# Feed-forward of a mixture of experts in halves of 1792 columns instead of quarters of 896, with two weight blocks of each half multiplied whole in float32

## The chip, the cores and the metric

The kernel runs on one core of one Trainium2 chip. The metric is the device time of one execution, in microseconds (us); lower is better.

## What is computed

Two layers over 272 tokens of width 1024 (16 fixed tokens ahead of the 256 of the input). Layer 0 ends in a dense feed-forward, layer 1 in a mixture of eight experts. The change touches the mixture alone:

```python
def swiglu(h, wg, wu, wd):
    return (jax.nn.silu(h @ wg) * (h @ wu)) @ wd

def moe_swiglu(h, router, wg, wu, wd):      # h: (1, 272, 1024); wg, wu: (8, 1024, 3584); wd: (8, 3584, 1024)
    logits = jnp.einsum('bld,de->ble', h, router).astype(jnp.float32)
    top_vals, top_idx = lax.top_k(logits, 2)
    top_w = jax.nn.softmax(top_vals, axis=-1)
    combine = jnp.sum(jax.nn.one_hot(top_idx, 8) * top_w[..., None], axis=-2)
    out = jnp.zeros_like(h)
    for e in range(8):
        out = out + combine[..., e:e + 1] * swiglu(h, wg[e], wu[e], wd[e])
    return out
```

The output is `rmsnorm(h + f)` of the last 256 tokens. All arrays are float32. Only those 256 tokens go through the mixture.

## The kernel before

**Precision.** TensorE is fed float32r, a rounded form of float32. Each weight block is therefore split in two: ScalarE (ACT) copies the raw block into a rounded first part (`whi`, line 149, `first_parts`), VectorE (DVE) subtracts it from the raw block and so makes the rest (`wlo`, line 157, `second_parts`). TensorE multiplies the tokens by both (`stream`, line 1089). The tokens of an expert are gathered into 128 places by a matmul with a selection matrix (`gather`, line 1028, plain float32). An expert with 64 tokens or fewer (few) has the rounded part of its tokens in the first 64 places of `exh` and the rest of them in the other 64, so that one pass over `whi` and `wlo` covers both; a small matmul by `fold` (line 1064) adds the lower half of the sums to the upper. An expert with more tokens (many) has all places filled, and after each unit of two blocks a branch (`tc.If(many > 0)`, line 1168) runs extra matmuls of `exl`, the tokens' rest, by `whi` (lines 1185 and 1205).

**Tiling.** The 3584 columns of an expert are done in `NS = 4` slabs of 896. A slab has four blocks of the gate and four of the up matrix (256 rows x 896 columns each, two row chunks side by side, so 1792 columns per partition), then the four blocks of the down matrix of the slab before (256 rows x 1024; the last 128 rows). Gate and up sums stand in a pair of PSUM banks each (`pgate`, `pup`), from a pool of three pairs (`rot`); the down sums of an expert stand in a pair of their own (`y`). When a sum is complete, ACT copies it to `part` for the fold (line 1060), TensorE folds, ACT computes Silu (line 1212), DVE the product with the up sums (line 1216); TensorE transposes the product (line 1075), and ACT and DVE split it again (`hh`, `hl`).

**Order.** Inside the mixture the order on TensorE, ACT and DVE is the program's. `unit` (line 1154) runs two blocks; at block m it first issues the first part of block m + 3 and the second part of block m + 1 (m + 2 for the last ten), and after a block it runs what `then(m, ...)` has hung there: folds, Silu, product, the gather of the next expert. Weight blocks are loaded by SyncE (line 101) into seven raw slots, in order; a slot is free once DVE has made the second part (`freed`). There are seven slots for `whi` and five for `wlo` (`NHI`, `NLO`).

**The end.** An expert's output is weighed into `yout` (`keep`, line 1095) and written to DRAM (`ydram`); in the last expert, `rows` (line 1136) gathers for each token the rows of the other seven from there, and DVE adds them to the residual `hsum` (line 1139).

Of the kernel before, what the change touches and what calls it, by code (L numbers as in the profile page):

```python
# [36 lines left out]
NSC = SLAB // P  # L37
ZROW = (NE - 1) * CAP
# [22 lines left out]
class Weights:  # L61
# [3 lines left out]
    def __init__(self, nc, blocks, slots):  # L65
# [11 lines left out]
        self.n_small = sum(blk[1] for blk in blocks[:self.first])  # L77
        self.n_hi = self.n_lo = 0
# [66 lines left out]
    def first_parts(self, j):  # L145
        while self.n_hi < min(j + 1, self.n_large):
            w, shaped = self.large(self.n_hi)
            hi = shaped(self.slot(self.n_hi % NHI, f"whi{self.n_hi}"))
            self.nc.scalar.activation(hi, w, AF.Copy)  # L149
            self.his[self.n_hi] = hi  # L150
            self.n_hi += 1

    def second_parts(self, j):
        while self.n_lo < min(j + 1, self.n_large):
            w, shaped = self.large(self.n_lo)
            lo = shaped(self.slot(NHI + self.n_lo % NLO, f"wlo{self.n_lo}"))
            self.nc.vector.tensor_sub(lo, w, self.his[self.n_lo].bitcast(F32))  # L157
            self.los[self.n_lo] = lo
            self.freed(self.first + self.n_lo)
            self.n_lo += 1  # L160
# [3 lines left out]
def tile_block(ctx, tc, x, meta_tokens, rel_bias, w_in, pool_group_w, w_pool_up, w_attn_up, w_out, dense_w_gate,  # L164
# [68 lines left out]
    def add_up(w, e, s):  # L233
        for b in range(4):
            src = w[0, e, b * 256:b * 256 + 256, s * SLAB:(s + 1) * SLAB]
            blocks.append((src.rearrange("(k p) f -> p k f", p=P), 1, None))

    def add_down(e, s, c0, m):
        for b in range((NSC + 1) // 2):
            r = s * SLAB + b * 256  # L240
            n = min(2, NSC - 2 * b)
            src = moe_w_down[0, e, r:r + n * P, c0:c0 + m]
            blocks.append((src.rearrange("(p k) f -> p k f", k=n), 1, None))
# [724 lines left out]
    def places():  # L968
        nc.vector.scalar_tensor_tensor(posb, few[:, None].to_broadcast([P, 2, NE]), float(HALF), pos, op0=ALU.mult,
                                       op1=ALU.add)  # L970

    def tables(pc_):
# [4 lines left out]
        nc.vector.tensor_scalar(big2, few, -1.0, 1.0, op0=ALU.mult, op1=ALU.add)  # L977
# [24 lines left out]
    exl = act.tile([P, 2, NCH, CAP], F32R, name="exl", tag="xl")  # L1002

    class Expert:


        def __init__(self, e):
# [9 lines left out]
            self.xh, self.xl = exh[:, e % 2], exl[:, e % 2]  # L1017
# [5 lines left out]
        def gather(self, cs=range(NCH)):  # L1023
            if cs[0] == 0:
                self.pg = two("pgat").rearrange("p h (c s) -> p (h c) s", s=CAP)
# [14 lines left out]
        def scales(self):  # L1040
            self.pst = bank("pst")
# [13 lines left out]
    def folded(E, ps):  # L1055
# [6 lines left out]
        def add():  # L1062
            for hf in range(2):
# [3 lines left out]
    def chunk(ci):  # L1067

        b, i = ci // 2, ci % 2
        return slice(b * 256 + i, (b + 1) * 256, 2) if ci < NSC - 1 else slice(b * 256, SLAB)  # L1070

    def turn(hs):
        pt = two("pth").rearrange("p h (c s) -> p (h c) s", s=P)[:, 0:NSC]
        for ci in range(NSC):
            nc.tensor.transpose(pt[:, ci], hs[:, chunk(ci)], ident)
        return pt
# [77 lines left out]
    def unit(bs, run, extra, many):  # L1154

        held = []
        m0 = step[0]
        for b in bs:
            m = step[0]
            ws.first_parts(m + AHEAD)  # L1160
            ws.second_parts(m + (1 if m < ws.n_large - 10 else 2))
            held.append(ws.his.pop(m))
            run(b, (held[-1], ws.los.pop(m)))
            if b != bs[-1]:
                for f in hooks.pop(m, ()):
                    f()
                step[0] += 1
        with tc.If(many > 0):  # L1168
            for b, hi in zip(bs, held):
                extra(b, hi)  # L1170
        for f in hooks.pop(step[0], ()):
            f()
        step[0] += 1

    def up(E, name):
        ps = two(name)
        outs = [(ps[:, hf, 0:SW], slice(hf * SW, (hf + 1) * SW)) for hf in range(2)]

        def run(b, parts):
            stream(outs, parts, [E.xh[:, 2 * b], E.xh[:, 2 * b + 1]], b == 0, b == 3)  # L1180

        def extra(b, hi):
            for i in range(2):
                for o, f in outs:
                    nc.tensor.matmul(o, E.xl[:, 2 * b + i], hi[:, i, f], start=False, stop=True, skip_group_check=True)

        for bs in ((0, 1), (2, 3)):
            unit(bs, run, extra, E.many)
        return ps[:, :, 0:SW]

    def down(E, s, h, hfs=(0, 1)):
# [4 lines left out]
        def chunks(b):  # L1196
            return range(2 * b, min(2 * b + 2, NSC))

        def run(b, parts):
            stream(outs, parts, [h[0][:, ci] for ci in chunks(b)], s == 0 and b == 0, s == NS - 1 and b == 3)  # L1200

        def extra(b, hi):
            for i, ci in enumerate(chunks(b)):
                for o, f in outs:
                    nc.tensor.matmul(o, h[1][:, ci], hi[:, i, f], start=False, stop=True, skip_group_check=True)

        for bs in ((0, 1), (2, 3)):
            unit(bs, run, extra, E.many)

    def gated(E, pg_, gs2, add):  # L1210
# [254 lines left out]
```

## Time and profile before

| | |
|---|---|
| three runs | 1563.52, 1564.65, 1564.68 us; median 1564.65 |
| profiled execution | 1566.1 us, its span 1564.3 us |
| mean granted TensorE clock | 0.986 of full speed |
| busy share of the span | TensorE matmul 94%, weight loads 82%, DVE 83%, ACT 69% |
| moved by DMA | 460.98 MB, mean 295 GB/s |

The mixture begins at about 616 us of the span and takes the rest of it. A stretch is read by its own rows: a matmul's duration includes the pipeline and overlaps the next, so that TensorE's pace is the distance from one start to the next, not the mean duration. A plain float32 matmul is recorded as two matmuls.

### The profile page before, as it was taken

The page shows a single profiled execution, that of the slowest core. Times are in us where ns is not written, and L with a number is a line of the kernel's source. Part 1 is how long each engine was busy: PE and PEld are TensorE (multiplying, and loading weights), DVE is VectorE, ACT ScalarE, POOL GpSimd, SP SyncE. Part 2 cuts the span into 40 slices and gives each one's busy share as a digit, 9 for nine tenths or more (in the row PEclk, how much of TensorE's full clock was granted, in tenths as well). Part 3 has the DMA queues.
Part 4 walks back from the last instruction along what each step waited for, and adds up shares of the span by engine and source line. Part 5 has one row for each costly group of instructions (what it writes and reads, how often), then busy time and mean ns, then how long its engine had stood idle before and what let it go on. Part 6 is the DMA issues. An engine that isn't in the chain of part 4 may idle for free. (4 is left out here: it accounts for less than half of the span.)

```text
span 1564.3 us, 22760 instructions
## 1 busy us (share of the span) xinstructions
PE 1469.2 (94%) x8667; PEld 1277.6 (82%) x8667; DVE 1306.1 (83%) x1429; ACT 1072.1 (69%) x1067; POOL 20.2 (1%) x27
## 2 busy tenths in 40 slices
PE   8999999999999997899899999999999999998785
PEld 7989999999999997677677888888776677676563
DVE  7766776666678677799999988878999999999896
ACT  5455554444455645878888767866888888887875
POOL 1000000000000000000000000000000000000100
PEclk9999999999999998999999999999999999999988
DMA  9734454555564336799999999999999999999994
GB/s 307 244 129 136 162 189 169 182 168 183 165 193 136 126 118 237 252 386 409 407 408 408 386 317 355 362 329 331 390 405 410 408 407 409 408 407 405 394 401 152
DMA packets 181266, 460.98 MB, mean 295 GB/s; under 512 B 10378, under 2 KB 83256, under 8 KB 169240
## 3 DMA queue, kind: packets, MB, share of 16 engines
q1 hardware_dynamic: 177328, 449.97, 77.5%
q0 software_dynamic: 2688, 9.24, 1.5%
q8 instruction: 81, 1.33, 0.3%
q14 instruction: 41, 0.34, 0.1%
q10 hardware_dynamic: 1128, 0.11, 0.1%
HBM read 453.49 MB, written 5.80 MB: 294 GB/s over the span
## 5 line engine op out<-in xcount | busy, mean ns | idle before, releaser
L157 DVE TENSOR_TENSOR wlo<-raw,whi 128x1792 fp32r<-128x1792 f32 (+2 forms) x388 | 753.1, 2001 | 28.0 <-ACT whi L149 25.1
L149 ACT ACTIVATE whi<-raw 128x1792 fp32r<-128x1792 f32 (+2 forms) x388 | 639.6, 1681 | 81.4 <-DMA raw<-in_moe_w_gate_dram 28.4
L125 ACT ACTIVATE w<-raw 128x1024 fp32r<-128x1024 f32 x180 | 189.7, 1058 | 251.1 <-PE ps L440 185.4
L126 DVE TENSOR_TENSOR w<-raw,w 128x1024 fp32r<-128x1024 f32 x180 | 219.5, 1223 | 66.4 <-ACT w L125 66.0
L440 PE MATMUL ps<-xh,w 128*128 128x272 f32 (+1 forms) x896 | 177.0, 293 | 0.5 <-ACT hT L761 0.5
L440 PE MATMUL ps<-fh,w 128*128 128x272 f32 x864 | 164.5, 290 | 0.0
L1089 PE MATMUL pgate<-wlo,exh 128*128 128x448 f32 x512 | 132.9, 382 | 22.5 <-DVE wlo L157 21.8
L440 PEld LDWEIGHTS ps<-xh,w 128*128 128x128 f32 x896 | 142.4, 190 | 4.2 <-PE s L502 1.1
L1089 PE MATMUL pgate<-whi,exh 128*128 128x448 f32 x512 | 133.0, 382 | 5.3 <-DVE exh L1036 1.8
L440 PEld LDWEIGHTS ps<-fh,w 128*128 128x128 f32 x864 | 135.7, 188 | 0.0
L1089 PE MATMUL pup<-whi,exh 128*128 128x448 f32 x512 | 127.8, 371 | 7.1 <-PEq L1168 6.0
L1089 PE MATMUL y<-wlo,hh 128*128 128x512 f32 x434 | 127.1, 408 | 6.8 <-DVE wlo L157 3.5
L1089 PEld LDWEIGHTS pgate<-wlo,exh 128*128 128x128 f32 x512 | 95.7, 193 | 44.6 <-DVE wlo L157 37.2
L1089 PE MATMUL pup<-wlo,exh 128*128 128x448 f32 x512 | 127.8, 371 | 2.2 <-DVE wlo L157 2.0
L440 PE MATMUL ps<-xl,w 128*128 128x272 f32 (+1 forms) x448 | 126.8, 288 | 0.0
L1089 PE MATMUL y<-whi,hh 128*128 128x512 f32 x434 | 122.8, 399 | 4.2 <-PEq L1168 1.5
L440 PE MATMUL ps<-fl,w 128*128 128x272 f32 x432 | 124.2, 288 | 0.0
L1089 PEld LDWEIGHTS pup<-whi,exh 128*128 128x128 f32 x512 | 95.0, 189 | 23.4 <-issue 13.7
L1089 PEld LDWEIGHTS y<-wlo,hh 128*128 128x128 f32 x434 | 77.0, 188 | 44.7 <-DVE wlo L157 30.0
L1089 PEld LDWEIGHTS pgate<-whi,exh 128*128 128x128 f32 x512 | 94.5, 193 | 20.9 <-issue 11.0
L1089 PEld LDWEIGHTS pup<-wlo,exh 128*128 128x128 f32 x512 | 93.5, 188 | 17.8 <-DVE wlo L157 10.3
L1089 PEld LDWEIGHTS y<-whi,hh 128*128 128x128 f32 x434 | 79.6, 188 | 27.3 <-issue 6.1
(315 smaller groups left out, 1995.3 us busy)
## 6 DMA issues: line engine op xcount, KB each, us to landing
raw<-in_moe_w_gate_dram SPq DMA_DIRECT2D x128, 896.0 KB, 8.9
raw<-in_moe_w_up_dram SPq DMA_DIRECT2D x128, 896.0 KB, 9.4
raw<-in_moe_w_down_dram SPq DMA_DIRECT2D x93, 1024.0 KB, 9.4
raw<-in_w_in_dram SPq DMA_DIRECT2D x30, 1024.0 KB, 6.3
raw<-in_moe_w_down_dram SPq DMA_DIRECT2D x37, 512.0 KB, 7.9
raw<-in_dense_w_gate_dram SPq DMA_DIRECT2D x14, 1024.0 KB, 5.0
raw<-in_dense_w_up_dram SPq DMA_DIRECT2D x14, 1024.0 KB, 4.9
raw<-in_dense_w_down_dram SPq DMA_DIRECT2D x14, 1024.0 KB, 5.0
```

What stands on the lines that cost most here:

```text
L125: self.nc.scalar.activation(hi, w, AF.Copy)
L126: self.nc.vector.tensor_sub(lo, w, hi.bitcast(F32))
L149: self.nc.scalar.activation(hi, w, AF.Copy)
L157: self.nc.vector.tensor_sub(lo, w, self.his[self.n_lo].bitcast(F32))
L440: newest[0] = nc.tensor.matmul(ps, w_[part][:, k, ms_], xp[:, k, sl], start=t == 0 and k == 0, stop=t == 2 and k == nk - 1).ins
L1089: nc.tensor.matmul(ps, x_, part[:, i, f], start=first and i == 0 and part is parts[0], stop=last and i == len(chunks) - 1 and part is part ...
```

## The change

- `NS` is 2: a half has 1792 columns. A gate or up block is now 128 rows x 1792 columns, eight of each to a half (as many bytes per block as before, one run of 7168 bytes per partition in place of two of 3584). A half has seven down blocks of 256 rows.
- The first gate and the first up block of each half are not split. They are multiplied from the raw block in plain float32, by `xf`, a float32 copy of the first 128 rows of the gathered tokens; no extra matmul runs for them. Their raw slot is free only when TensorE is done (`freed` in `unit`).
- Sums of a half need four PSUM pairs: `pgate0`, `pgate1`, `pup0`, `pup1`, from the same pool of three; `pup1` takes the pair of `pgate0`, and Silu of `pgate0` is done in two parts. The first up unit runs its two blocks piece by piece with the fold and Silu of `pgate0` in between.
- `NLO` is 4, second parts are always made two blocks ahead. The tail's `rows` and their additions are hung at other places.

The core of the diff:

```diff
-NS = 4
+NS = 2
-NRAW, NRAWE, NPAIR, NHI, NLO, AHEAD = 6, 2, 5, 7, 5, 3
+NRAW, NRAWE, NPAIR, NHI, NLO, AHEAD = 6, 2, 5, 7, 4, 3
-SLAB = DFF // 4
-SW = SLAB // 2
+SLAB = DFF // 2
+SW = SLAB // 4
...
     def add_up(w, e, s):
-        for b in range(4):
-            src = w[0, e, b * 256:b * 256 + 256, s * SLAB:(s + 1) * SLAB]
-            blocks.append((src.rearrange("(k p) f -> p k f", p=P), 1, None))
+        for b in range(NCH):
+            src = w[0, e, b * P:(b + 1) * P, s * SLAB:(s + 1) * SLAB]
+            blocks.append((src.rearrange("(k p) f -> p k f", p=P), 1 if b else 0, None))
...
         def first(self, cs=slice(0, NCH)):
             nc.scalar.activation(self.xh[:, cs], self.pg[:, cs], AF.Copy)
+            if cs.start == 0:
+                nc.scalar.activation(self.xf[:, 0:HALF], self.pg[:, 0, 0:HALF], AF.Copy)
+                nc.scalar.activation(self.xf[:, HALF:], self.pg[:, 0, HALF:], AF.Copy,
+                                     scale=big2[:, self.e:self.e + 1])
...
+    def unit(bs, runs, extra, many):
+        m0 = step[0]
         held = []
         for b in bs:
+            m = m0 + b - bs[0]
             ws.first_parts(m + AHEAD)
-            ws.second_parts(m + (1 if m < ws.n_large - 10 else 2))
+            ws.second_parts(m + 2)
+            if m in ws.whole:
+                held.append((ws.large(m)[0], None))
+            else:
+                held.append((ws.his.pop(m), ws.los.pop(m)))
+            if len(runs) == 1:
+                runs[0](b, held[-1])
+                if m in ws.whole:
+                    ws.freed(ws.first + m)
...
+        if len(runs) > 1:
+            for run in runs:
+                run(bs, held)
+            for i in range(len(bs)):
+                if m0 + i in ws.whole:
+                    ws.freed(ws.first + m0 + i)
...
+        def block(b, parts, outs):
+            w, lo = parts
+            if lo is None:
+                for o, f in outs:
+                    nc.tensor.matmul(o, E.xf, w[:, 0, f], start=b == 0, stop=b == NCH - 1)
+            else:
+                stream(outs, parts, [E.xh[:, b]], b == 0, b == NCH - 1)
...
+                runs = [some(outs[0:2], 0), call(between[0]), some(outs[0:2], 1), call(between[1])]
+                for o in outs[2:4]:
+                    runs += [some([o], 0), some([o], 1)]
+            unit((b, b + 1), runs, extra, E.many)
...
+            if end:
+                then(mg + 2, lambda: added.append(rows(0)))
+                then(mg + 7, lambda: (added[0](), added.append(rows(1))))
+                then(mg + 11, lambda: added[1]())
+            pg_ = [two("pgate0"), two("pgate1")]
+            up(E, sums(pg_[0], 0) + sums(pg_[1], 1))
...
+            def first_gate(E=E, ps=pg_[0], gs2=gs2[0], add=add_g):
+                for hf in range(2):
+                    gated(E, ps, gs2, add, (hf,))
...
+            up(E, sums(pu[0], 0) + sums(pu[1], 1), (first_gate, lambda: None))
...
+            if prev is None:
+                turn_part(0, md)
+                turn_part(1, md + 1)
+            else:
+                then(md + 3, lambda f=turn_part: f(0, md + 4))
+                if end:
+                    then(md + 5, lambda f=turn_part: f(1, mt))
+                down(prev[0], prev[1], turned)
+                if not end:
+                    turn_part(1, mt)
+                if prev[1] == NS - 1:
+                    add_y = folded(prev[0], prev[0].y)
+                    then(mt + 1, add_y)
+                    then(mt + 2, lambda E=prev[0]: keep(E, E.e))
```

How the order moves, at the two places that the prediction speaks of. The first is the step from the last gate block to the first up unit, in the middle of the mixture. TensorE before, the end of the first up unit and the fold of the gate sums behind it:

```order
L1089 MATMUL pup<-whi_8762,exh 128x448 [waits Activation_49]
L1089 MATMUL pup<-whi_8762,exh 128x448 x3
L1089 MATMUL pup<-wlo_8805,exh 128x448 [waits DVE_49]
L1089 MATMUL pup<-wlo_8805,exh 128x448 x3
L1168 COMPARE_AND_BRANCH
L1185 MATMUL pup<-whi_8739,exl 128x448 x4
L1185 MATMUL pup<-whi_8762,exl 128x448 x4
L1168 UNCONDITIONAL_BRANCH
L1168 UNCONDITIONAL_BRANCH [waits PE_49]
L1064 MATMUL pgate<-part,fold 128x448 [waits Activation_49]
L1064 MATMUL pgate<-part,fold 128x448
```

TensorE with the change, the first up unit itself (`pup_8931` is `pup0`, `pup_8932` is `pup1` in the banks of `pgate_8790`, which is `pgate0`):

```order
L1208 MATMUL pup_8931<-raw_8796,exf 128x448 [waits DMAHW3_49,PE_49]
L1208 MATMUL pup_8931<-raw_8796,exf 128x448
L1074 MATMUL pgate_8790<-part,fold 128x448 [waits Activation_49] x2
L1099 MATMUL pup_8931<-whi_8897,exh 128x448 x2
L1099 MATMUL pup_8931<-wlo_8909,exh 128x448 [waits DVE_49]
L1099 MATMUL pup_8931<-wlo_8909,exh 128x448
L1208 MATMUL pup_8932<-raw_8796,exf 128x448 [waits Activation_49]
L1099 MATMUL pup_8932<-whi_8897,exh 128x448
L1099 MATMUL pup_8932<-wlo_8909,exh 128x448
L1208 MATMUL pup_8932<-raw_8796,exf 128x448
L1099 MATMUL pup_8932<-whi_8897,exh 128x448
```

ACT before, at the same step (`part` is the copy of the gate sums, `gs` is Silu):

```order
L1060 ACTIVATE part<-pgate 128x2x448
L149 ACTIVATE whi_10574<-raw_10449 128x1792
L1168 UNCONDITIONAL_BRANCH
L149 ACTIVATE whi_10588<-raw_10495 128x2048
L1212 ACTIVATE gs<-pgate,rcs 128x896
```

ACT with the change:

```order
L1070 ACTIVATE part<-pgate_8790 128x2x448 [waits PE_49]
L154 ACTIVATE whi_8935<-raw_8829 128x1792 [waits DMAHW5_49,DVE_49]
L154 ACTIVATE whi_8941<-raw_8843 128x1792 [waits DMAHW6_49,DVE_49]
L1254 ACTIVATE gs<-pgate_8790,rcs 128x448 [waits PE_49] x2
L1070 ACTIVATE part<-pgate_8791 128x2x448 [waits Activation_49]
```

ACT's order is the same, with two first parts between `part` and Silu. What moved is TensorE: before, nothing of the up block waited for Silu; now the first matmul into `pup1` waits for ACT in the middle of the unit.

The second place is the last expert, where the gathered rows are added to the residual. ACT before (`yout<-y` is the output of expert 6):

```order
L149 ACTIVATE whi_14279<-raw_14192 128x1792
L1095 ACTIVATE yout<-y,rcs 128x1024
L149 ACTIVATE whi_14304<-raw_14218 128x1792
L1168 UNCONDITIONAL_BRANCH
L149 ACTIVATE whi_14318<-raw_14232 128x1792
```

DVE before, up to the first two additions:

```order
L1079 TENSOR_TENSOR hl<-pth,hh 128x896
L1081 SCALAR_TENSOR_TENSOR hh<-hl,few,hh 128x7x64
L157 TENSOR_TENSOR wlo_14528<-raw_14403,whi_14479 128x1792
L157 TENSOR_TENSOR wlo_14551<-raw_14429,whi_14510 128x1792
L157 TENSOR_TENSOR wlo_14565<-raw_14443,whi_14526 128x1792
L1168 UNCONDITIONAL_BRANCH
L157 TENSOR_TENSOR wlo_14592<-raw_14469,whi_14549 128x1792
L157 TENSOR_TENSOR wlo_14606<-raw_14483,whi_14563 128x1792
L1139 TENSOR_TENSOR hsum<-hsum,yout 128x1024
L1168 UNCONDITIONAL_BRANCH
L1139 TENSOR_TENSOR hsum<-hsum,exl 128x1024
```

ACT with the change:

```order
L154 ACTIVATE whi_14008<-raw_13894 128x1792
L154 ACTIVATE whi_14022<-raw_13911 128x1792
L154 ACTIVATE whi_14043<-raw_13942 128x1792
L1105 ACTIVATE yout<-y,rcs 128x1024
L1193 UNCONDITIONAL_BRANCH
```

DVE with the change:

```order
L163 TENSOR_TENSOR wlo_14063<-raw_13942,whi_14043 128x1792
L1193 UNCONDITIONAL_BRANCH
L163 TENSOR_TENSOR wlo_14086<-raw_13977,whi_14061 128x1792
L163 TENSOR_TENSOR wlo_14098<-raw_14012,whi_14084 128x1792
L1193 UNCONDITIONAL_BRANCH
L163 TENSOR_TENSOR wlo_14131<-raw_14026,whi_14119 128x1792
L1193 UNCONDITIONAL_BRANCH
L1149 TENSOR_TENSOR hsum<-hsum,yout 128x1024
L1149 TENSOR_TENSOR hsum<-hsum,exl 128x1024
```

With the change three second parts stand between the one that belongs to the first part ahead of `yout` (`whi_14043`) and the first addition. Before, there are thirteen between the one that belongs to the first part behind `yout` (`whi_14304`) and the first addition.

## Rows read from the trace of the kernel before

**Rows 1.** Busy time by stretch: us, then PE, PEld, DVE, ACT, POOL, clock, DMA, GB/s.

```profile
1131.07:1404.76 273.69, 251.76 (x1148) 192.94 (x1147) 269.98 (x171) 238.33 (x169) 1.06 (x2) 1.00 1.02 408
866.01:1122.57 256.56, 254.31 (x1237) 221.04 (x1236) 216.95 (x137) 189.17 (x135) 1.06 (x2) 1.00 0.94 349
616.00:650.00 34.00, 27.57 (x121) 23.13 (x122) 21.46 (x29) 17.97 (x14) 0.51 (x1) 0.89 0.47 157
```

**Rows 2.** Timeline of ACT: Silu of two slabs, ten apart; output of two experts, two apart.

```profile
1131.07 1.01 ACT L1212 ACTIVATE gs<-pgate,rcs 128x896 f32<-128x896 f32 x1
...
1404.76 0.99 ACT L1212 ACTIVATE gs<-pgate,rcs 128x896 f32<-128x896 f32 x1
...
866.01 1.10 ACT L1095 ACTIVATE yout<-y,rcs 128x1024 f32<-128x1024 f32 x1
...
1122.57 1.12 ACT L1095 ACTIVATE yout<-y,rcs 128x1024 f32<-128x1024 f32 x1
```

**Rows 3.** DMA packets, 1217 to 1227 us (gate, up), then 1208 to 1212 us (down).

```profile
DMA packets 1196, 4.04 MB, mean 404 GB/s; under 512 B 68, under 2 KB 68, under 8 KB 1196
...
DMA packets 231, 1.69 MB, mean 422 GB/s; under 512 B 25, under 2 KB 25, under 8 KB 25
```

**Rows 4.** Timeline of DVE: seven second parts in a row (start, us).

```profile
1513.43 13.90 DVE L157 TENSOR_TENSOR wlo<-raw,whi 128x1792 fp32r<-128x1792 f32 x7
```

**Rows 5.** TensorE groups, 1131.07 to 1404.76 us: count, busy us, mean ns, idle before.

```profile
L1089 PE MATMUL y<-wlo,hh 128*128 128x512 f32 x140 | 41.1, 409 | 1.6 <-DVE wlo L157 0.5
...
L1089 PE MATMUL pgate<-wlo,exh 128*128 128x448 f32 x160 | 40.8, 377 | 7.6 <-DVE wlo L157 7.3
...
L1028 PE MATMUL pgat<-s,h2g 128*128 128x128 f32 x96 | 11.2, 275 | 0.0
L1075 PE MATMUL pth<-cst,gs 128*128 128x128 f32 x70 | 10.7, 292 | 1.5
```

**Rows 6.** Timeline of TensorE in an expert with many tokens.

```profile
910.12 1.79 PE L1185 MATMUL pup<-whi,exl 128*128 128x448 f32 x8
911.75 0.57 PE L1064 MATMUL pgate<-part,fold 128*128 128x448 f32 x2
...
920.75 2.03 PE L1205 MATMUL y<-whi,hl 128*128 128x512 f32 x8
922.62 0.57 PE L1064 MATMUL pup<-part,fold 128*128 128x448 f32 x2
```

**Rows 7.** Timeline of TensorE across the end of a unit, an expert with few tokens.

```profile
1527.65 0.99 PE L1089 MATMUL pup<-wlo,exh 128*128 128x448 f32 x4
1528.79 1.17 PE L1089 MATMUL y<-whi,hh 128*128 128x512 f32 x4
```

**Rows 8.** Timeline of TensorE: plain float32 matmuls, 16 of 128 columns, one of 272.

```profile
1144.69 3.74 PE L1028 MATMUL pgat<-s,h2g 128*128 128x128 f32 x32
...
27.33 0.62 PE L411 MATMUL pr<-ss,ones 128*128 128x272 f32 x2
```

**Rows 9.** Timeline of ACT after the last gate block, an expert with many tokens.

```profile
907.08 0.92 ACT L1060 ACTIVATE part<-pgate 128x896 fp32r<-128x896 f32 x1 [3.95 <-PE pgate L1185]
907.89 3.50 ACT L149 ACTIVATE whi<-raw 128x1792 fp32r<-128x1792 f32 x2
912.35 1.01 ACT L1212 ACTIVATE gs<-pgate,rcs 128x896 f32<-128x896 f32 x1 [0.96 <-PE pgate L1064]
```

**Rows 10.** From the output of expert 6 to its gathered rows: ACT, POOL; median us to landing.

```profile
1453.33 1.11 ACT L1095 ACTIVATE yout<-y,rcs 128x1024 f32<-128x1024 f32 x1
...
1464.35 3.07 POOL L1136 DMA_INDIRECT yout<-ydram,rows_of  x1 [9.06 <-DMA ydram<-yout]
1467.72 2.58 POOL L1136 DMA_INDIRECT exl<-ydram,rows_of  x1 [0.30 <-issue]
...
yout<-ydram,rows_of POOLq DMA_INDIRECT x2, 9.2
exl<-ydram,rows_of POOLq DMA_INDIRECT x2, 9.0
```

More of the change, by code (lines that the diff above doesn't have):

```diff
@@ L77, in __init__ @@
         self.n_small = sum(blk[1] for blk in blocks[:self.first])
+        self.whole = {j for j, blk in enumerate(blocks[self.first:]) if blk[1] == 0}
+        self.parted = [j for j in range(self.n_large) if j not in self.whole]
         self.n_hi = self.n_lo = 0
@@ L1069, in chunk, with turn @@
         b, i = ci // 2, ci % 2
[L1070 to L1075, printed above, removed]
+        return slice(b * 256 + i, (b + 1) * 256, 2)
+    def turn(hs, cis):
+        pt = two("pth").rearrange("p h (c s) -> p (h c) s", s=P)[:, 0:len(cis)]
+        for i, ci in enumerate(cis):
+            nc.tensor.transpose(pt[:, i], hs[:, chunk(ci)], ident)
         return pt
@@ L1175, in up @@
[L1175 to L1180, printed above, removed]
-        def extra(b, hi):
[L1183 to L1189, printed above, removed]
+            ws.second_parts(m + 2)
@@ new lines, in unit, with up, some, call @@
+        with tc.If(many > 0):
+            for b, (hi, lo) in zip(bs, held):
+                if lo is not None:
+                    extra(b, hi)
+        step[0] += len(bs)
+        for f in hooks.pop(step[0] - 1, ()):
+            f()
+    def up(E, outs, between=None):
+        def block(b, parts, outs):
[5 more added lines that the diff above has]
+                stream(outs, parts, [E.xh[:, b]], b == 0, b == NCH - 1)
+        def extra(b, hi):
+            for o, f in outs:
+                nc.tensor.matmul(o, E.xl[:, b], hi[:, 0, f], start=False, stop=True, skip_group_check=True)
+        for b in range(0, NCH, 2):
+            runs = [lambda b, parts: block(b, parts, outs)]
+            if b == 0 and between is not None:
+                def some(os, i):
+                    return lambda bs, held: block(bs[i], held[i], os)
+                def call(f):
+                    return lambda bs, held: f()
+                runs = [some(outs[0:2], 0), call(between[0]), some(outs[0:2], 1), call(between[1])]
+                for o in outs[2:4]:
+                    runs += [some([o], 0), some([o], 1)]
+            unit((b, b + 1), runs, extra, E.many)
@@ L1191, in down, with sums @@
+    def sums(ps, i):
+        return [(ps[:, hf, 0:SW], slice((2 * i + hf) * SW, (2 * i + hf + 1) * SW)) for hf in range(2)]
     def down(E, s, h, hfs=(0, 1)):
@@ L1269, in tile_block @@
-            if add_y is not None:
-                then(m1, add_y)
-                then(m1 + 1, lambda E=prev[0]: keep(E, E.e))
+            if s == NS - 1 and e + 1 < NE:
+                then(mg + 3, made[-1].folds)
+            if end:
[4 more added lines that the diff above has]
+            up(E, sums(pg_[0], 0) + sums(pg_[1], 1))
@@ new lines, in tile_block, with part_g @@
+            gs = mb.tile([P, SLAB], F32, name="gs")
+            gs2 = [gs[:, i * 2 * SW:(i + 1) * 2 * SW].rearrange("p (h f) -> p h f", h=2) for i in range(2)]
+            pu = [two("pup0"), two("pup1")]
+            add_g = folded(E, pg_[0][:, :, 0:SW])
+            def first_gate(E=E, ps=pg_[0], gs2=gs2[0], add=add_g):
+                for hf in range(2):
+                    gated(E, ps, gs2, add, (hf,))
+            def part_g(E=E, ps=pg_[1], gs2=gs2[1]):
+                add = folded(E, ps[:, :, 0:SW])
+                then(mu + 3, lambda: gated(E, ps, gs2, add))
@@ L1288, in tile_block @@
+            turned = parts
             prev = (E, s)
```

176 lines of the change are left out of this document (85 added, 91 removed).

## Prediction

> **What bounds the kernel now.** I cut the mixture into stretches by the output of each expert and read the busy time of each stretch first [rows 1]. Experts 0, 1 and 4 to 7 have few tokens, 2 and 3 many, and these two kinds have different limits.
>
> In ten slabs of few-token experts [rows 2] one Silu follows the other by 273.69 / 10 = 27.37 us, so what will be one half takes 54.74 us now. Here DMA is at its limit (share 1.02, 408 GB/s) and DVE nearly so (269.98 of 273.69 us busy, 54.0 per half). TensorE's 251.76 us look close as well, but durations overlap. Its pace comes from starts: eight 448-column matmuls from 910.12 to 911.75 are 0.204 us each, eight of 512 columns from 920.75 to 922.62 are 0.234 [rows 6]. The durations of the same groups, 1.79 and 2.03 us, show a tail of 0.16 us behind the last. With that tail taken off, a 128-column float32 record takes (3.74 - 0.16) / 32 = 0.112 us [rows 8]. The counts [rows 5] then give, for ten slabs: 640 matmuls into gate and up (four groups of 160) 130.6 us, 280 into y (two of 140) 65.5, 96 gather records and 70 transposes at 0.112 18.6, 40 folds 8.2; together 222.9, or 44.6 per half. Between units TensorE stands still: four matmuls from 1527.65 end at 1528.47 by that pace, the next start is 1528.79 [rows 7], so 0.32 us, and 12 units to a half make 3.8. TensorE needs 48.4 of 54.74 us: some 6 us to spare.
>
> In the two experts with many tokens [rows 1, 2] one takes 256.56 / 2 = 128.3 us, and PE is busy 254.31 of 256.56. TensorE is the limit, DVE has 15% free, DMA little less than before. What TensorE gains or loses there counts in full.
>
> **The change, part by part.**
>
> *Longer rows.* In gate and up a 3584-byte packet occupies an engine 16 x 10 us / 1128 = 141.8 ns (1196 packets less 68 small ones), in down an 8192-byte packet 16 x 4 / 206 = 310.7 ns [rows 3]. A straight line through both gives 10.8 ns fixed and 0.0366 ns per byte, so 273 ns for 7168 bytes against 283.7 for two of 3584: 3.7% less. Sixteen gate and up blocks of 256 such packets take 16 x 256 x 141.8 / 16 ns = 36.3 us of a half, so 1.4 us go. DMA alone then asks for 54.7 - 1.4 = 53.3 us per half. No row shows a 7168-byte packet; the ends are no gain, and the down rows' 422 against 404 GB/s, 1.6 us.
>
> *Two blocks not split.* DVE loses two second parts of 13.90 / 7 = 1.99 us [rows 4], so it falls from 54.0 to 50.0 us per half and is no limit any more. ACT loses two first parts of 3.50 / 2 = 1.75 us [rows 9]; it had 3.5 us free per slab [rows 1], and the two small copies for `xf` once per expert vanish in that.
>
> *Two blocks in float32.* By the 128-column record (0.112) and the 272-column one, (0.62 - 0.16) / 2 = 0.23 [rows 8], a record grows by 0.82 ns per column; at 448 columns that is 0.375, and a float32 matmul is two records, 0.75 us. A whole block is four of them, 3.0 us. Few tokens: before, 8 x 0.204 = 1.63, so +1.37, twice: +2.7 us per half. Many tokens: the extra pass goes too, before 12 x 0.204 = 2.45, so +0.55, twice: +1.1. The page "FP8 and Floating Point Precision" of the Trainium skill (TensorE Precision Notes) speaks against the change here: true float32 is four passes through the array. Four passes at the split matmuls' pace would be 0.82 per matmul and 3.3 per block, some 0.5 us more per half; the gather's record agrees nearly (a 128-column float32 matmul takes 0.22 us).
>
> *A new wait.* Before, nothing in the up blocks needed Silu. Now the first matmul into `pup1` needs the banks of `pgate0`, thus the first half of its Silu, and on ACT two first parts stand ahead of that. Count from the end of the gate sums. ACT: in 907.08 to 911.39 `part` and the two first parts [rows 9], 4.3 us, then half of a Silu of 1.01: 4.8. TensorE meanwhile has two float32 matmuls (1.5), the fold (0.41) and four matmuls of block 1 (0.8): 2.7. It waits 2.1 us, and behind this wait stands everything on TensorE, it being one queue. Ends: 0 if the two first parts were done early, 2.6 if Silu must be complete.
>
> *Few tokens, per half.* TensorE 48.4 + 2.7 + 2.1 = 53.2; DMA 53.3. Two resources at the same limit that wait for each other lose something: before, a half took 54.74 with packets worth 36.3 + 17.4 (7 down blocks of 1.05 MB at 422 GB/s), a loss of 1.0, with TensorE 6 us from the limit. With no room there I add 0.9 to 53.3: 54.2, or -0.5. Eleven such halves (all but the last): **-5.5 us**. Ends: -15 if DMA alone sets the pace (-1.4 each), +7 if the loads stand still while TensorE waits (53.3 + 2.1, +0.7 each).
>
> *Many tokens.* +1.1 + 2.1 = 3.2 per half, four halves: **+12.8**. Ends: +4.4 without the wait, +15 with 3.3 us per block.
>
> *The start, 616 to 650 us.* DMA is far from its limit (157 GB/s) and PE at 27.57 of 34.00 [rows 1]. One `wlo` slot fewer, a raw slot held longer, and the first half's `up` later: **0**, plus or minus 5, a seventh of the stretch being the most that one slot in seven can move.
>
> *The last half.* From the start of expert 6's `yout` to the first gathered rows it takes 1464.35 + 9.2 - 1453.33 = 20.2 us, to the second 1467.72 + 9.0 - 1453.33 = 23.4 [rows 10]. Before, thirteen second parts (26 us) stood between, and nobody waited. Now it is three, 6 to 8 us, so DVE will stand some 12 us and more at the first addition, with all second parts behind it. TensorE has two blocks of second parts, 2 x 54.74 / 23 = 4.8 us, so it loses 12 + 3 - 5, about 10, and the loads part of it once all slots are full. Some comes back since DVE is faster now: **+9**, ends +3 and +13.
>
> *At nothing:* the earlier second parts (two blocks ahead) lie in DVE's new 4 us; the next half's gate sums find their banks free, because seven down blocks, over 13 us, stand between.
>
> Sum: -5.5 + 12.8 + 0 + 9 = +16.3 on the profiled 1566.1, 1582.4; this execution stands 1.45 above the median of the runs, so **1581 us** against 1564.65.
>
> **Rivals.**
>
> *Faster: the wait is hidden and DMA sets the pace.* Decided by how long TensorE waits for Silu: below 1.4 us, TensorE is under 52.5 in a half, far enough below DMA's 53.3. Then few -15, many +4.4, last half +3: -8, **1557**. For it: DMA's share of 1.02 is the firmest limit, and DVE and ACT, its helpers, get 4 us of room each. Against it: the two first parts ahead of Silu stand in ACT's order, and 4.3 us for them is measured.
>
> *No gain from DMA.* The whole blocks' raw slots stay taken until TensorE is done with them, about two blocks (4.8 us) longer than if DVE freed them. One slot in seven for 4.8 us, twice a half, is 1.4 us of loads, as much as the rows bring. Then few 0: +22, **1586**. Longer rows that bring nothing would give the same. The Trainium skill's page "DMA: Bandwidth & Descriptors" (Specifications) asks for 512 bytes only for line rate, by which both row lengths are alike; 404 against 422 GB/s speaks for the gain, though no run here has 7168-byte rows.
>
> *The sums cancel:* few -12, many +8, last +5, within 0.2%, 3.1 us, about what a measurement of this kernel can tell from no change: 1565. That the change doesn't do what it says I rule out, as the order shows two first and second parts fewer in each half and the float32 matmuls in their place.
>
> **How the numbers follow.** Forecast 0.49, with its own range 1569 to 1592; DMA sets the pace 0.27; no gain 0.15; cancelled 0.09. So faster by over 0.2% is 0.27, within it 0.09, slower 0.64. The low end, 1553, takes the faster rival with 4 us from the start; the high end is few +4, many +15, last half +13: +32, 1597.
>
> **What would show it.** Right: DVE busy in the few-token stretch about 50 of 54 us, a wait of TensorE for ACT of some 2 us at the first matmul into `pup1` in each half; GB/s above 410 while gate and up move, in packets of 7168 bytes; outputs of the many-token experts 134 to 135 us apart; a half of the others 54 us; a DVE wait of over 10 us at the first addition to `hsum`. Wrong: no wait at `pup1` and halves of 53.3 us (the faster rival); halves of 54.7 or more with raw slots as the releaser of the loads; many-token experts less than 130 us apart; float32 matmuls of 448 columns far from 0.75 us from start to start.

## The result, and the profile after

The change takes **1656.87 us** (median of four runs, 1654.99 to 1658.62) against 1564.19 for the kernel before: 1.0593 times as long, 95% interval 1.0574 to 1.0611. Forecast were 1581 us and a range of 1553 to 1597. The sign was right, but the forecast rise of 16 us was less than a fifth of the measured one.

To see where the 93 us stand, I cut each trace at the first gate matmul of every half (before: of every second slab). The sums of these distances, from the profiled executions:

| stage | forecast | before | after | difference |
|---|---|---|---|---|
| eleven halves with few tokens | -5.5 | 601.5 | 656.2 | **+54.7** |
| four halves with many tokens | +12.8 | 257.9 | 275.6 | +17.7 |
| last half, to the end of the span | +9 | 88.4 | 106.0 | +17.6 |
| up to the mixture | 0 | 616.5 | 615.8 | -0.7 |

The seven halves from expert 4 to the first of expert 7, as the windows view gives them: before

```profile
1090.39:1475.90 385.51, 351.08 (x1577) 267.66 (x1576) 373.63 (x234) 331.17 (x235) 8.51 (x7) 1.00 1.02 403
```

and after (columns as in [rows 1]):

```profile
1124.21:1547.57 423.36, 374.22 (x1589) 285.41 (x1587) 345.79 (x212) 307.57 (x226) 2.31 (x4) 0.96 0.94 365
```

DVE is less busy by 27.8 us, four per half, as forecast, and ACT by 23.6. But no engine is at a limit any more: TensorE is busy in 374 of 423 us, DMA's share fell from 1.02 to 0.94 and its rate from 403 to 365 GB/s, and the granted clock from 1.00 to 0.96. A stretch in which everything has got emptier is one of waits. Two stand out: one in each half, and one at the gather of the next expert's tokens, in seven of the sixteen halves. What TensorE waited for there in the whole mixture (total us, times, longest):

```profile
PE pgate L1074 <- ACT gs L1254: 54.1, 16, 5.3
PE pnext L1034 <- DVE s L1019: 12.7, 6, 3.0
```

Of the seven gathers four wait for 3.0 us; the other three wait for 0.5 us or less.

**The wait in each half.** TensorE in the first up unit of expert 5's second half; in brackets the idle time before and its releaser:

```profile
1324.57 1.74 PE L1208 MATMUL pup<-raw,exf 128*128 128x448 f32 x4 [0.30 <-PEq L1193]
1326.38 0.47 PE L1074 MATMUL pgate<-part,fold 128*128 128x448 f32 x1
1330.93 0.74 PE L1074 MATMUL pgate<-part,fold 128*128 128x448 f32 x1 [4.09 <-ACT gs L1254]
```

ACT in the same stretch:

```profile
1325.42 0.90 ACT L1070 ACTIVATE part<-pgate 128x896 fp32r<-128x896 f32 x1
1326.27 1.70 ACT L154 ACTIVATE whi<-raw 128x1792 fp32r<-128x1792 f32 x1
1328.66 1.70 ACT L154 ACTIVATE whi<-raw 128x1792 fp32r<-128x1792 f32 x1 [0.69 <-DMA raw<-in_moe_w_up_dram]
1330.26 0.62 ACT L1254 ACTIVATE gs<-pgate,rcs 128x448 f32<-128x448 f32 x1
1331.71 0.63 ACT L1254 ACTIVATE gs<-pgate,rcs 128x448 f32<-128x448 f32 x1 [0.83 <-PE pgate L1074]
```

TensorE doesn't wait at `pup1`, where the prediction had put it, but earlier: the *second* fold of `pgate0` waits for the Silu of the first half of the same pair. That Silu stands behind two first parts, and one of these waits for its load as well. The clock in these 14 us, in steps of 2:

```profile
1326.00:1328.00 2.00, 0.78 (x2) 0.19 (x1) 1.58 (x2) 1.97 (x2) 0.00 (x0) 1.00 0.99 406
1328.00:1330.00 2.00, 0.00 (x0) 0.00 (x0) 2.00 (x1) 1.34 (x1) 0.00 (x0) 0.93 1.03 430
1330.00:1332.00 2.00, 1.07 (x3) 0.99 (x4) 1.64 (x2) 1.17 (x3) 0.00 (x0) 0.50 1.01 419
1332.00:1334.00 2.00, 2.00 (x7) 1.45 (x5) 0.41 (x1) 2.00 (x3) 0.00 (x0) 0.50 1.04 428
1334.00:1336.00 2.00, 2.00 (x5) 1.08 (x5) 0.00 (x0) 2.00 (x2) 0.00 (x0) 0.50 1.00 416
1336.00:1338.00 2.00, 1.85 (x7) 1.12 (x6) 0.70 (x1) 0.32 (x1) 0.00 (x0) 0.86 1.05 434
1338.00:1340.00 2.00, 2.00 (x11) 1.81 (x11) 2.00 (x2) 0.00 (x0) 0.00 (x0) 1.00 0.98 406
```

While TensorE stands, for 4.1 us, the granted clock falls to 0.50 (1.2 GHz). It stays there for nearly 7 us, more than 5 of them with TensorE at work again; from 1338 it is back at 1.00 (2.4 GHz).

**The wait at the gather**, between the up and the down blocks of a half in which the next expert's tokens are gathered. TensorE after the last up block of expert 6's first half:

```profile
1403.52 0.97 PE L1099 MATMUL pup<-wlo,exh 128*128 128x448 f32 x4
1407.47 5.44 PE L1034 MATMUL pnext<-s,h2g 128*128 128x128 f32 x32 [2.99 <-DVE s L1019]
...
1414.61 0.56 PE L1074 MATMUL pup<-part,fold 128*128 128x448 f32 x2
```

and DVE beside it:

```profile
1400.23 6.43 DVE L163 TENSOR_TENSOR wlo<-raw,whi 128x1792 fp32r<-128x1792 f32 x3 [2.97 <-ACT whi L154]
1406.57 0.53 DVE L1019 TENSOR_SCALAR s<-cst,pos,sel 128x64 f32<-128x64 f32 x2
1407.02 0.53 DVE L1019 TENSOR_SCALAR s<-cst,posb,sel 128x64 f32<-128x64 f32 x2
1407.47 2.28 DVE L163 TENSOR_TENSOR wlo<-raw,whi 128x2048 fp32r<-128x2048 f32 x1
1415.28 1.15 DVE L1258 SCALAR_TENSOR_TENSOR gs<-pup,rcs,gs 128x896 f32<-128x896 f32 x1 [5.53 <-PE pup L1074]
```

The selection matrix `s` is made right before its use now, on DVE, behind three second parts that are issued two blocks ahead. DVE reached them late, too, as it had stood 3.0 us for a first part of ACT. TensorE waits 3.0 us for `s`, then gathers in part at the low clock (5.44 us against 3.74 [rows 8]; the row for 1406 to 1412 below has a mean clock of 0.72); the fold of the up sums stands behind the gather; and DVE, whose product needs that fold, stands 5.5 us with all second parts behind it. No raw slot comes free meanwhile, and the loads stop:

```profile
1406.00:1412.00 6.00, 4.53 (x26) 4.56 (x27) 3.75 (x6) 2.20 (x2) 0.00 (x0) 0.72 1.01 411
1414.00:1420.00 6.00, 5.85 (x27) 4.53 (x26) 4.68 (x4) 5.02 (x6) 0.00 (x0) 1.00 0.18 43
1420.00:1432.00 12.00, 10.94 (x49) 7.71 (x48) 11.96 (x9) 6.69 (x6) 0.00 (x0) 1.00 0.82 280
```

Before, `s` was made in the middle of the slab that ends in the gather. DVE's row, and TensorE's first and last start of the gather, some 15 us later:

```profile
1347.05 0.54 DVE L1013 TENSOR_SCALAR s<-cst,pos,sel 128x64 f32<-128x64 f32 x2
```

```profile
L1028 PE MATMUL pgat<-s,h2g x32: 275/275/275, 1362.7 to 1366.2; 128*128 128x128 f32 x32
```

**The last half.** DVE at the additions of the gathered rows:

```profile
1575.26 1.23 DVE L1149 TENSOR_TENSOR hsum<-hsum,yout 128x1024 f32<-128x1024 f32 x1 [8.42 <-DMA yout<-ydram,rows_of]
1578.68 1.23 DVE L1149 TENSOR_TENSOR hsum<-hsum,exl 128x1024 f32<-128x1024 f32 x1 [2.20 <-DMA exl<-ydram,rows_of]
...
1590.28 1.23 DVE L1149 TENSOR_TENSOR hsum<-hsum,exl 128x1024 f32<-128x1024 f32 x1 [1.49 <-DMA exl<-ydram,rows_of]
```

8.4 + 2.2 + 1.5 = 12.1 us: the wait that was forecast, though only 8.4 of it stand at the first addition, where over 10 were expected. It explains a part of the 17.6 (below).

### The profile page after: what moved, and what is told of

Its sections match the earlier page's. It is cut to its first block, busy times and chain, and to the rows that moved or that the text cites. A ratio compares the mean times of both kernels' runs of the same rounds, so it can differ in the third digit from the quotient of the medians.

```text
span 1653.5 us, 22542 instructions
## 1 busy us (share of the span) xinstructions
PE 1519.8 (92%) x8635; PEld 1299.3 (79%) x8635; DVE 1245.9 (75%) x1384; ACT 1019.1 (62%) x1054; POOL 18.1 (1%) x27
## 5 line engine op out<-in xcount | busy, mean ns | idle before, releaser
L163 DVE TENSOR_TENSOR wlo<-raw,whi 128x1792 fp32r<-128x1792 f32 (+2 forms) x343 | 694.7, 2067 | 158.7 <-ACT whi L154 115.4
L154 ACT ACTIVATE whi<-raw 128x1792 fp32r<-128x1792 f32 (+2 forms) x343 | 576.3, 1734 | 70.3 <-DMA raw<-in_moe_w_up_dram 43.4
L1099 PE MATMUL pup<-whi,exh 128*128 128x448 f32 x448 | 140.4, 425 | 3.6
L1099 PE MATMUL pgate<-whi,exh 128*128 128x448 f32 x448 | 117.6, 384 | 4.5
L1099 PE MATMUL pgate<-wlo,exh 128*128 128x448 f32 x448 | 109.8, 367 | 0.2 <-DVE wlo L163 0.2
L1099 PEld LDWEIGHTS pgate<-whi,exh 128*128 128x128 f32 x448 | 81.8, 188 | 27.1 <-issue 16.1
L1254 ACT ACTIVATE gs<-pgate,rcs 128x448 f32<-128x448 f32 (+1 forms) x48 | 36.3, 756 | 91.9 <-PE pgate L1074 91.9
L445 PE MATMUL ps<-hh,w 128*128 128x272 f32 x448 | 85.7, 290 | 0.0
L445 PEld LDWEIGHTS ps<-xl,w 128*128 128x128 f32 x448 | 84.2, 190 | 0.7 <-issue 0.4
L1074 PE MATMUL pgate<-part,fold 128*128 128x448 f32 x64 | 29.9, 509 | 59.1 <-ACT gs L1254 54.1
```

Of the source, the lines that this page charges most:

```text
L163: self.nc.vector.tensor_sub(lo, w, self.his[q].bitcast(F32))
L445: newest[0] = nc.tensor.matmul(ps, w_[part][:, k, ms_], xp[:, k, sl], start=t == 0 and k == 0, stop=t == 2 and k == nk - 1).ins
L1074: nc.tensor.matmul(ps[:, hf], E.fold, part[:, hf, 0:n], start=False, stop=True, skip_group_check=True)
L1099: nc.tensor.matmul(ps, x_, part[:, i, f], start=first and i == 0 and part is parts[0], stop=last and i == len(chunks) - 1 and part is part ...
L1254: nc.scalar.activation(gs2[:, hf], ps[:, hf, 0:SW], AF.Silu, scale=E.rc[:, 0:1])
```

## The experiments

Theory A (order): the loss comes from the two waits and from what they set off (the low clock, DVE behind the product, loads that stop). Theory B (slots): the whole blocks keep raw slots until TensorE is done with them, and the loads starve.

**All blocks split** (`allsplit`): four blocks more per expert are split, the rest is the change.

```diff
-            blocks.append((src.rearrange("(k p) f -> p k f", p=P), 1 if b else 0, None))
+            blocks.append((src.rearrange("(k p) f -> p k f", p=P), 1, None))
```

> All sixteen blocks of a half are split as the others are; halves, order and hooks are those of the change. Order theory (the loss comes from waits at Silu and at the gather, whole blocks have little part in it): the waits stay, DVE gets its 4 us per half back, TensorE loses 2.7; within 25 us of the change, 1635 to 1680. Slot theory (raw slots held until TensorE is done starve the loads): most of the loss goes, 1590 to 1610, and the loads of few-token experts run above 405 GB/s throughout.

Measured 1657.43 us, as the change (1.0587, 1.0554 to 1.0619). While the waits stand, the whole blocks cost or give nothing that the intervals could show. Theory B in this form is out.

**Silu ahead of the first parts** (`silu_first`): in the first up unit the two first parts, and the second parts with them, are issued behind both folds and Silu.

```diff
+                add()
                 for hf in range(2):
-                    gated(E, ps, gs2, add, (hf,))
+                    gated(E, ps, gs2, lambda hfs: None, (hf,))
...
-            ws.first_parts(m + AHEAD)
-            ws.second_parts(m + 2)
+            if len(runs) == 1:
+                ws.first_parts(m + AHEAD)
+                ws.second_parts(m + 2)
...
-            for run in runs:
+            for i, run in enumerate(runs):
                 run(bs, held)
+                if i == 1:
+                    for m in (m0, m0 + 1):
+                        ws.first_parts(m + AHEAD)
+                        ws.second_parts(m + 2)
```

> The change with Silu of pgate0 ahead of the two first parts on ACT, and both folds ahead of Silu on TensorE. Order theory: the 3.6 to 5.4 us that TensorE stands at the second fold fall below 1 us, and with them the slow clock behind it (some 2.5 us more); sixteen halves at 4 to 7 us are 64 to 112 us, of which the loads give back no more than down to 53.3 us per half, so 1590 to 1620. Slot theory: TensorE only waits elsewhere, for the loads; within 15 us of the change.

Measured 1601.76 us: 55.1 less than the change (1.0254, 1.0224 to 1.0283).

**Only the folds together** (`folds_only`): the part of that diff ahead of its first `...` alone; the first parts stay ahead of Silu.

> The change with only the two folds of pgate0 brought together ahead of Silu; the two first parts stay ahead of Silu on ACT. If the wait at the second fold (instead of at pup1, where the prediction had it) is what made it larger: 1.0 us of TensorE work comes ahead of the wait in each of sixteen halves, with less slow clock behind it: 16 to 35 us faster than the change, 1622 to 1641. If first parts that wait for their loads set the time of Silu whatever TensorE does: the same wait ends at the same time; within 10 us of the change.

Measured 1640.83 us, 16 less (1.0498, 1.0474 to 1.0522). Here the wait is at `pup1`, where the prediction had put it. It is 2.05 us in the half below, and 41.4 / 16 = 2.6 us in the mean of all halves, against 2.1 forecast:

```profile
1130.75 1.74 PE L1208 MATMUL pup<-raw,exf 128*128 128x448 f32 x4 [0.30 <-PEq L1193]
1131.98 0.92 PE L1074 MATMUL pgate<-part,fold 128*128 128x448 f32 x2
...
1135.76 1.02 PE L1208 MATMUL pup<-raw,exf 128*128 128x448 f32 x2 [2.05 <-ACT gs L1254]
...
PE pup L1208 <- ACT gs L1254: 41.4, 16, 4.3
```

The order with the folds together is the one that the prediction had reckoned with, and it is still 77 us slower than before. So the misplaced wait explains 16 us of the miss and no more.

**Selection matrix early** (`early_s`):

```diff
+            if s == 0 and e + 1 < NE:
+                then(mu + 3, lambda e=e: made.append(Expert(e + 1)))
...
-                    made.append(Expert(e + 1))
                     made[-1].gather(pair_=extra_pair)
```

> The change with the selection matrix of the next expert made on DVE four blocks earlier, so that the gather need not wait for it behind second parts. Order theory: the 3.0 us wait and the slow clock of the gather (5.4 against 3.7 us) go in seven halves, and DVE's wait for the product behind it is shorter; 4 to 8 us in each of seven halves, 28 to 56, unless the Silu wait takes it back: 1600 to 1640. Slot theory: within 15 us of the change.

Measured 1630.45 us, 26.4 less than the change (1.0413, 1.039 to 1.0436). That is more than the 12.7 us that TensorE had waited for `s`; the low clock and the stop of the loads go with the wait. At the place where the loads had stopped in the change, behind the gather of expert 6's first half, they now move 328 GB/s:

```profile
1402.00:1408.00 6.00, 5.85 (x26) 4.50 (x26) 5.21 (x5) 5.25 (x4) 0.00 (x0) 1.00 0.90 328
```

**Both** (`silu_early`):

> Both of these edits together. Order theory: what is left is TensorE at 51 us and DMA at 53.3 us per half of a few-token expert, 1.1 us per half more in the many-token ones and the waits of the last half; 1565 to 1590. Slot theory: above 1620.

Measured 1582.75 us (1.0116, 1.0097 to 1.0135): 74.1 of the 93 us are gone with two moves of instructions that take no work away. The two effects alone (55.1 and 26.4) add up to 81.5, so they overlap little. The seven halves of above, with the clock back at 0.99:

```profile
1088.05:1477.12 389.07, 364.13 (x1589) 277.30 (x1588) 346.12 (x212) 309.00 (x226) 2.31 (x4) 0.99 0.98 396
```

TensorE's wait at `pup1` is now

```profile
1331.49 1.02 PE L1213 MATMUL pup<-raw,exf 128*128 128x448 f32 x2 [0.43 <-ACT gs L1259]
```

What remains against the kernel before was taken apart from this one.

**Without whole blocks** (`split_early`: `silu_early` with the diff of `allsplit`):

> Silu first, selection matrix early, and all blocks split: no float32 blocks. If the whole blocks cost more than they give (TensorE 1.1 us per half of a many-token expert, 2.7 per half of a few-token one, their raw slots held longer): 4 to 20 us faster than with them, 1563 to 1579. If they pay (two second parts fewer per half, 4 us of DVE, which otherwise stands at 54 us of a half of 55): 5 to 20 us slower, 1588 to 1603.

Measured 1571.04 us (1.0048, 1.0031 to 1.0065). Now the whole blocks cost 11.7 us.

**Whole blocks from a copy** (`copied`): ACT copies the raw block in plain float32 into the slot of a first part, and the raw slot is free at once.

```diff
+            if q in self.whole:
+                hi = hi.bitcast(F32)
             self.nc.scalar.activation(hi, w, AF.Copy)
...
+            if q in self.whole:
+                self.freed(self.first + q)
...
-                held.append((ws.large(m)[0], None))
+                held.append((ws.his.pop(m), None))
```

> Silu first, selection matrix early, whole blocks still multiplied in float32, but from a copy that ACT makes (plain float32, in the slot of a first part), so that the raw slot is free as soon as ACT is done; DVE still does nothing for them. Without whole blocks this kernel takes 1571.0, with them from the raw slot 1582.8. If the whole blocks cost through their raw slots: 1568 to 1575. If they cost through TensorE's float32 passes: 1579 to 1584.

Measured 1573.5 us (1.0069, 1.0053 to 1.0086). Of the 11.7 us 9.3 were the raw slots. The other 2.5, which the float32 passes cost net of what DVE saves, are not clear of the intervals; the traces have them in the many-token halves (261.0 against 258.7 us), while the few-token halves are alike (592.2). What the DMA queue waited for in the seven halves, of `silu_early` (total us, times, longest)

```profile
SPq L105 <- PE pgate L1213: 22.1, 7, 7.3
...
SPq L105 <- PE pup L1213: 5.0, 2, 2.5
```

has no TensorE in it with the copy; in a like stretch

```profile
SPq L105 <- DVE wlo L167: 297.9, 134, 6.5
...
SPq L105 <- ACT whi L156: 3.7, 6, 1.6
```

**The last half**: `rows_late` hangs the additions of `silu_early` at the last half's blocks 11 and 18 instead of 7 and 11; `rows_wide` also loads the first four of its seven down blocks in full width; `split_rows_late` and `split_rows_wide` are the same without whole blocks.

```diff
-                then(mg + 7, lambda: (added[0](), added.append(rows(1))))
-                then(mg + 11, lambda: added[1]())
+                then(mg + 11, lambda: (added[0](), added.append(rows(1))))
+                then(mg + 18, lambda: added[1]())
```

```diff
-    for hf in range(2):
-        add_down(NE - 1, NS - 1, hf * 512, 512)
+    add_down(NE - 1, NS - 1, 0, D, range(NWIDE))
+    for hf in range(2):
+        add_down(NE - 1, NS - 1, hf * 512, 512, range(NWIDE, NDB))
```

> Silu first, selection matrix early, and the additions of the gathered rows in the last half hung four and seven blocks later. If DVE's wait for the rows (12 us in three pieces in the change) is what the last half loses: 8 to 13 us faster than without this edit, 1570 to 1575. If the last half is longer for another reason (the longer down part at the end, the product chain): within 3 us, 1580 to 1586.

Measured 1577.72 us, 5.0 less than `silu_early`: a miss, as it lies between the two ranges, so the additions are a part of the loss and not most of it. DVE no longer waits at the additions; in the trace the last half falls from 104.3 to 98.5 us.

> Silu first, selection matrix early, late additions, and the first four of the seven down blocks of the last half loaded in full width instead of in two column halves. The last half took 98.5 us with late additions against 88.4 before the change. If the narrow blocks at the end cost the rest: 4 to 8 us faster than the 1577.7 without this edit, 1570 to 1574. If the chain of the product behind the last up block does: within 3 us of it.

Measured 1573.49 us, 4.2 less again; the last half is 95.0 us, against 88.4 before the change.

> All three edits and no whole blocks. The two effects add up if they have different places: the sum of the two differences to the kernel with Silu first and the selection matrix early, within 4 us. If DVE is what both relieve, less than the sum.

Measured 1568.49 us: 14.3 less than `silu_early`, where 11.7 and 5.0 make 16.7; that is within 4 of the sum but below it, so the two expectations are not told apart.

> The same without whole blocks: 1568.5 without the wide blocks, so 1561 to 1565 if the narrow blocks cost 4 to 8 us, as fast as the kernel before; 1566 to 1570 if they cost nothing.

Measured 1564.49 us, as the kernel before (1.0011, 0.9999 to 1.0022).

**The product one block later** (`split_wide_late`: the last one, with the first product at `md + 1` and the second at `md + 3`):

> The last one with the fold and product of the up sums hung one block later, behind which TensorE waited 1.8 us with slow clock in some halves: 2 to 8 us faster than it if those waits are still on the path, 0 to 2 if the loads set the pace of the few-token halves.

Measured 1560.02 us (0.9983, 0.9973 to 0.9992): 4.5 less.

**All together, with float32 blocks** (`copied_wide_late`), **and the same with the first wait put back** (`silu_last`: the first up unit in the change's order):

> All mended edits (Silu first, selection matrix early, late additions, wide down blocks, late product) and the float32 blocks multiplied from ACT's copy. Without float32 blocks this took 1560.0. If only the many-token experts pay for the float32 passes (0.6 to 1.1 us in each of four halves): 1562 to 1565. If DVE's 4 us per half are worth something now: 1556 to 1560. If TensorE is the limit of few-token halves too: 1568 or more.

Measured 1560.6 us (0.9983, 0.9974 to 0.9991), between the first two ranges and no different from the version without float32 blocks.

> The same, but in the first up unit Silu stays behind the two first parts on ACT and the second fold behind Silu, as in the change. If the wait alone costs what the first experiments gave (1630.5 less 1582.8, 48 us, with the selection matrix early in both): 40 to 55 us slower than copied_wide_late. If most of that came from raw slots that stay taken while TensorE waits: 10 to 30 us.

Measured 1609.96 us (1.0303, 1.0288 to 1.0318): 49.4 more, 3.1 per half, with no raw slot held for TensorE. TensorE's waits for Silu, here and then in `copied_wide_late`:

```profile
PE pgate L1080 <- ACT gs L1256: 46.0, 16, 4.1
...
PE pup L1215 <- ACT gs L1261: 6.9, 16, 0.5
```

So 39.1 us more of waiting cost 49.4 us.

By stage, in us from the traces (the difference to before in brackets):

| | few, 11 halves | many, 4 halves | last half |
|---|---|---|---|
| before | 601.5 | 257.9 | 88.4 |
| the change | 656.2 (+54.7) | 275.6 (+17.7) | 106.0 (+17.6) |
| `silu_early` | 600.6 (-0.9) | 261.0 (+3.1) | 104.3 (+15.9) |
| `copied` | 592.2 (-9.3) | 261.0 (+3.1) | 103.1 (+14.7) |
| `split_early` | 592.2 (-9.3) | 258.7 (+0.8) | 104.6 (+16.2) |
| `rows_wide` | 600.1 (-1.4) | 261.9 (+4.0) | 95.0 (+6.6) |
| `split_wide_late` | 588.5 (-13.0) | 256.8 (-1.1) | 97.0 (+8.6) |
| `copied_wide_late` | 588.8 (-12.7) | 260.0 (+2.1) | 94.9 (+6.5) |
| `silu_last` | 621.3 (+19.8) | 274.9 (+17.0) | 96.2 (+7.8) |

## Why the prediction was wrong

**The step that failed** is the term "Few tokens, per half", -0.5 us, which came out at +5.0. Two things went into it wrongly, the place of the wait for Silu and what a wait costs in the sum, and one was left out.

*Left out: the gather's selection matrix.* The prediction priced the earlier second parts "at nothing", because they lie in DVE's new room. They do by DVE's busy time. But DVE works in the program's order, and the change makes `s` right before the gather, so that what is ahead of it on DVE became a wait of TensorE, and then one of DVE for TensorE. I had followed the moved instructions at two places only and not at this third one, although the diff shows both lines. Undoing it gives 26.4 us alone (`early_s`), and 19.0 where the other wait is mended (`silu_early` against `silu_first`).

*Wrong: what the Silu wait costs.* Its mechanism (two first parts ahead of Silu on ACT) was right. Its place was the second fold and not `pup1`: in the order's "fold [waits Activation] x2" I took both waits to be for `part`. In seven halves of the changed kernel

```profile
PE pgate L1074 <- ACT gs L1254: 25.2, 7, 5.3
```

it is 25.2 / 7 = 3.6 us in place of 2.1; `folds_only` shows 16 us for the place, all halves together. The larger error is in the sum. I let 2.1 us of waiting fit into a half that DMA bounds at 53.3 us. But a wait on TensorE cost its length and more here: most of these waits have the low clock behind them, and the time is not made up later. `silu_last` prices this in a kernel without the other waits, 3.1 us per half; its few-token halves, which DMA was to bound, lose (621.3 - 588.8) / 11 = 3.0 us each. That TensorE can't catch up because its own work, 51 us by the prediction's count, leaves little room in a half of 53 is only argued.

*Right: the loads.* Where loads run freely, 6 us of the changed kernel show

```profile
DMA packets 402, 2.55 MB, mean 425 GB/s; under 512 B 46, under 2 KB 46, under 8 KB 402
```

so 16 x 6 / (402 - 46) = 270 ns per 7168-byte packet, where 273 was forecast. The Trainium skill's page "DMA: Bandwidth & Descriptors" (Specifications), by whose 512-byte bound both row lengths would be alike, is not borne out: 425 GB/s against the 404 of [rows 3]. The gain shows only once nothing else stops the loads, and is smaller than the 1.4 us per half that were taken: -9.3 us in `copied`, 0.85 per half, and -13.0 in `split_wide_late`, 1.2. These kernels differ from the one before in more than the rows, so not all of it need be theirs.

**Many tokens**, +12.8: measured +17.7. Without the waits it is +3.1 (`silu_early`), so the float32 passes and the rest are 0.8 per half (forecast 1.1) and the waits 3.7 (forecast 2.1). Right in mechanism, the wait too small: each is 2.6 us long here, and what it costs is more than its length.

**The float32 block.** Forecast 0.75 us per matmul, 3.0 per block. The gate block shows eight records, four matmuls, with the matmuls of the next block behind them:

```profile
1308.08 3.17 PE L1208 MATMUL pgate<-raw,exf 128*128 128x448 f32 x8
1310.74 1.32 PE L1099 MATMUL pgate<-whi,exh 128*128 128x448 f32 x4
1311.90 0.97 PE L1099 MATMUL pgate<-wlo,exh 128*128 128x448 f32 x4
```

The start of the `whi` row, 2.66 us behind the block's, is no measure: its first record begins while the last float32 matmul still runs, and the row lasts 1.32 us where the `wlo` row lasts 0.97. Up to the start of `wlo` it is 3.82 us, and less four split matmuls of 0.204 [rows 6] that leaves 3.0 per block, 0.75 per matmul, as forecast; (3.17 - 0.16) / 8 = 0.376 per record says the same. By the four passes of the Trainium skill ("FP8 and Floating Point Precision", TensorE Precision Notes) it would be 4 x 0.204 = 0.82, an estimate; the measurement is a little lower, 3.7 times the split matmul, and decides here.

**The last half**, +9: measured +17.6. The rows' wait came as forecast (12.1 us on DVE), but hanging the additions later, which ends it, gives only some 5 us (`rows_late`). The narrow down blocks were not in the sum at all: the down part behind the last up block is twice as long with halves, all in column halves, and loading four blocks in full width gives 4.2 us, and 4.0 in the pair without whole blocks. The 6.5 us that stay in `copied_wide_late` were not taken apart; that half an expert's down work is left after the last product, where before it was a quarter, is only argued.

**The rivals.** "No gain from DMA" had the right mechanism, the raw slots, at 1.4 us per half; `copied` against `silu_early` gives 8.4 us in eleven halves, 0.8 each. It is hidden while the larger waits stand, as `allsplit` shows. The faster rival, halves that DMA alone paces, is what the mended versions come near: 588.8 / 11 = 53.5 us per half against 53.3. Its total, 1557, is 3.6 below the measured 1560.6, though that is with other edits in the last half.

## What to carry to other kernels

Follow every instruction that changes its place, on each engine, to what stands ahead of it in that engine's queue; one microsecond of DVE work moved behind three long instructions cost 19 to 26 us here, more than the 13 us that the few-token halves gain in the best version. A wait on a nearly full TensorE cost more than its length (49.4 us for 39.1), so price the slow matmuls behind it as well, and don't let it vanish in another resource's limit. And an edit whose parts seem to be worth nothing (`allsplit`) may only be covered by a larger wait: price it again once that is gone.

The version that came out best keeps halves and float32 blocks from a copy, or splits all blocks, with Silu ahead of the first parts, `s` made four blocks earlier, later additions and product, and wide down blocks. It takes 1560.0 to 1560.6 us, 0.17% less than the kernel before (interval 0.9973 to 0.9992), so the gain of all this work is small. Whether the later product would help the kernel before was not tried, and neither were `NLO` at 5 or second parts one block ahead in the halves.

## What the runs showed of the hardware that was not expected

The granted clock fell to 0.50 (1.2 GHz) while TensorE stood for 4.1 us, and stayed there for more than 5 us of work. It fell at the gather too, at a wait of 3.0 us: 32 records took 5.44 us, in `silu_early` 3.81. Shorter waits brought it in some halves and not in others: in the four many-token halves of the change TensorE waits 2.6 us for Silu each time, and the mean clock is 1.00 in the first half and 0.98 in each of the other three.

DMA's busy share is no sure measure of what it moves. From 1290 to 1300 us of the changed kernel its share was 0.63, and it moved

```profile
DMA packets 331, 2.09 MB, mean 209 GB/s; under 512 B 40, under 2 KB 40, under 8 KB 331
```

which is half of the 425 GB/s above at more than half of the share there, 1.02. Two short stretches of the same kernel have nearly the same share at 272 and 419 GB/s:

```profile
1318.00:1320.00 2.00, 2.00 (x12) 1.85 (x11) 2.00 (x3) 2.00 (x2) 0.00 (x0) 1.00 0.92 272
1380.00:1382.00 2.00, 2.00 (x12) 1.79 (x10) 2.00 (x2) 0.53 (x1) 0.00 (x0) 1.00 1.00 419
```

What sets such stretches apart is not shown: the loads' queue waits for slots near both.
